# Differences of the down projection's weights, formed beside the up projection instead of beside the input projection

## The chip, the cores and the metric

The kernel runs on one core of one Trainium2 chip. A core has five engines, each with an instruction stream of its own that runs strictly in order: TensorE (PE in the profile, matrix products), VectorE (DVE), ScalarE (ACT), GpSimd (POOL) and SyncE (SP), which here issues every DMA transfer. An instruction that waits for a semaphore holds up everything behind it on its own engine. Products land in PSUM, all other tiles lie in SBUF; the large arrays lie in HBM. The metric is the device time of one execution in microseconds, as the median of several runs.

## The reference

One decoder layer over 1040 tokens of width 1024: an input projection, differential attention and an HGRN2 recurrence side by side, an output projection, and a feed-forward network with a short convolution. The last is what the change touches:

```python
def conv_ffn(a, w_up, conv_w, conv_b, w_down):
    u = a @ w_up
    C = u.shape[-1]
    u = lax.conv_general_dilated(
        u, conv_w[:, None, :].astype(u.dtype), window_strides=(1,),
        padding=[(CONV_WIDTH - 1, 0)], dimension_numbers=('NWC', 'WIO', 'NWC'),
        feature_group_count=C) + conv_b
    gate, up = jnp.split(u, 2, axis=-1)
    return (jax.nn.gelu(gate, approximate=True) * up) @ w_down
```

`w_down` has 2816 rows and 1024 columns.

## The kernel before

Every operand of a large product is split into a high part `hi` and a low remainder `lo` (`split`, lines 146 to 149: ScalarE rounds, VectorE or GpSimd subtracts), and each product is three matmuls: hi by hi, hi by lo, lo by hi.

The stages follow each other: the normalised input and first projections; then, head by head, the rest of the input projection (`dense`, line 742) interleaved with attention (`attn`) and the recurrence (`hgrn_head`); the output projection; the up projection with convolution and gate; the down projection. In the profile the input projection with its heads runs from about 52 to 500 us, the up projection from about 684 to 1150 us, the down projection to the end.

The up and the down projection each use Strassen's scheme with seven products in place of eight. It needs sums and differences of quarters of both operands. In the down projection (lines 1375 to 1548) the weights of products 5, 6, 7 and 4 are such differences. They depend on the weights alone, so they are formed ahead of time and kept in a scratch array `tsc` in HBM, from where `w_in` (line 1395) reads them. The rows of `w_down` are taken in 11 pairs of blocks of 128 rows, `k` and `k + 11`; for each `k` four tiles of 128x512 (`11`, `12`, `22`, `21`: 256 KB each) are loaded, four subtractions are made on VectorE in place, and the four results are stored. That is `down_sums` (lines 184 to 203). It is a generator: `dense` takes one step of it ahead of each group of the input projection (line 749), and the first step of a `k` loads, the next four subtract and store. Its tiles `wd` lie in the pool `wsp` with six buffers, which the output projection later uses for its weights.

The up projection runs over `ft` = 0 to 21, blocks of 128 gate columns and 128 up columns; `ft` = 0 is done without Strassen. For each other `ft` there are seven products `j` = 0 to 6, and for each of them two units `p` = 0 and 1, halves of the tokens. One unit's product is 12 matmuls. `unit` (lines 1291 to 1330) uses three PSUM banks, `pa`, `pb` and `pc`, that take several products each. Product 1 goes into `pb`, VectorE forms `u2 = pb + x1`, and product 3 adds into the same bank; then VectorE forms `u3 = pb + x1` and product 5 adds again. So product 3 waits for u2 and product 5 for u3. At the end `gated` (line 1265) runs the convolution `c` (ScalarE once, VectorE twice, for each side), the gate on ScalarE, a product on GpSimd and a store to `gsc` in HBM. `prep` (line 1078) makes the weights of the product seven places ahead: it loads four tiles `ra` for each `ft` (five buffers), forms sums `ws` on GpSimd and splits them into `uh` and `ul`, the `ul` on VectorE for `j` = 0, 1, 3, 5 and on GpSimd for `j` = 2, 4, 6.

The pool `dn` ("down", line 1360) is opened before the up projection. Its tag `gk` has four buffers of 128x512, which the down projection's `g_in` (line 1390) uses for tiles `gi` that it reads from `gsc`; the results of splitting these are `gh` and `gl`.

TensorE's order is that of the program. For the other engines and for SP's transfers a scheduler sets the order when the kernel is built: it takes the earliest instruction in program order that is ready by its own reckoning, so later work is drawn ahead where buffers are free. Through this the first four `gi` tiles of the down projection, with their `gh` and `gl`, stand in `ft` = 1 to 4 of the up projection.

## Time and profile before

| | |
|---|---|
| median of three runs | 1342.56 us (1341.45 to 1344.93) |
| the profiled execution | 1337.75 us |
| its span, first to last instruction | 1336.0 us |
| mean granted TensorE clock | 0.995 |
| TensorE busy | 1289.1 us, 96% of the span |
| VectorE busy | 909.6 us, 68% |
| ScalarE busy | 693.4 us, 52% |
| GpSimd busy | 435.4 us, 33% |
| loads of `wd`, 44 of 256 KB | issued from 52.0 to 343.8 us |
| subtractions of `wd`, 44 | from 58.1 to 352.3 us |
| stores to `tsc`, 44 of 256 KB | issued from 58.7 to 378.7 us |

Rows of the timeline give the start in us, the busy time in us, engine, line, operation, output and inputs by the program's names, their shapes and the count of instructions merged; in square brackets stands how long the engine had been idle before, and what ended that. L53 is the line of a helper that records every instruction of VectorE, ScalarE and GpSimd, so these are told apart by tiles. Rows of groups give a count, the busy time, the mean of one in ns, and the idle time ahead. Rows of waits give the total in us, the number of times and the longest. "To landing" is the time from the issue of a transfer until its semaphore shows it done. A matmul's busy time overlaps that of its neighbours.

### The profile page before, as it was taken

To read this page: it belongs to the slowest core of one execution; us is meant where nothing else is said; L and a number is where in the kernel's file an instruction comes from. 1 tells how busy PE (TensorE), PEld (TensorE's weight loads), DVE (VectorE), ACT (ScalarE), POOL (GpSimd) and SP (SyncE) were. 2 spreads that over 40 slices of the span, in tenths; PEclk is the share of its full clock that TensorE was granted. 3 is DMA by queue.
4 is the path that set the end of the run, shared out by engine and by line. 5 is a ranking of instruction groups with operands and counts; after the bars stand their busy time and mean duration, and the time that the engine had idled before them with its cause. 6 is when DMAs were issued, how large, how long until landed. Compare 5 with 4: busy or idle time off the path is not lost.

```text
span 1336.0 us, 26153 instructions
## 1 busy us (share of the span) xinstructions
PE 1289.1 (96%) x10172; PEld 1186.8 (89%) x10172; DVE 909.6 (68%) x1530; ACT 693.4 (52%) x1633; POOL 435.4 (33%) x340
## 2 busy tenths in 40 slices
PE   7999999999999998999999999999999999999997
PEld 6899999989999998677899999999999998888875
DVE  6675657574746464637798777787787776697586
ACT  7465456535654665237674454444445444454553
POOL 5211212021212110326045666656666630010121
PEclk9999999999999999999999999999999999999999
DMA  5331343144311223567512222123222225954253
GB/s 207 115 134 64 116 145 124 56 140 135 111 49 58 75 88 134 187 189 254 197 48 88 88 95 73 72 95 104 80 87 72 76 92 195 340 182 166 87 205 118
DMA packets 99425, 164.99 MB, mean 123 GB/s; under 512 B 10035, under 2 KB 34899, under 8 KB 99302
## 3 DMA queue, kind: packets, MB, share of 16 engines
q1 hardware_dynamic: 99302, 163.32, 35.9%
q8 instruction: 80, 1.31, 0.4%
q14 instruction: 43, 0.35, 0.1%
HBM read 122.65 MB, written 40.63 MB: 122 GB/s over the span
## 4 chain that ended last, share of the span: by engine, by line
PE 48%; DVE 5%; issue 3%; DMA 2%; POOL 2%; ACT 2%; SPq 0%; DVEq 0%; POOLq 0%; ACTq 0%
PE pd L1461 5%; PE pd L1462 5%; PE pd L1460 5%; PE pb L1302 4%; PE pb L1304 4%; PE pb L1303 4%; PE pc L1302 2%; PE pc L1303 2%; PE pa L1302 2%; PE pa L1304 2%; PE pc L1304 2%; PE pa L1303 2%; PE py L982 1%; PE py L978 1%; PE py L980 1%
## 5 line engine op out<-in xcount | busy, mean ns | idle before, releaser
L1302 PE MATMUL pb<-t,uh 128*128 128x258 f32 x504 | 143.0, 284 | 4.6 <-DVE u L53 4.5
L1303 PE MATMUL pb<-t,uh 128*128 128x258 f32 x504 | 141.7, 281 | 0.0
L1304 PE MATMUL pb<-t,ul 128*128 128x258 f32 x504 | 141.6, 281 | 0.0
L1461 PE MATMUL pd<-wl,gh 128*128 128x512 f32 x308 | 121.9, 396 | 0.1
L1460 PE MATMUL pd<-wh,gh 128*128 128x512 f32 x308 | 121.7, 395 | 0.0
L1462 PE MATMUL pd<-wh,gl 128*128 128x512 f32 x308 | 121.7, 395 | 0.0
L53 DVE SCALAR_TENSOR_TENSOR c<-uu,cwt,c 128x514 f32<-128x514 f32 (+1 forms) x88 | 97.0, 1102 | 20.6 <-ACT c L53 19.9
L53 POOL TENSOR_TENSOR c<-c,c 128x514 f32<-128x514 f32 (+1 forms) x44 | 63.4, 1441 | 122.7 <-ACT c L53 120.0
L1302 PEld LDWEIGHTS pb<-t,uh 128*128 128x128 f32 x504 | 95.4, 189 | 6.1 <-DVE u L53 5.8
L1303 PEld LDWEIGHTS pb<-t,uh 128*128 128x128 f32 x504 | 95.5, 189 | 0.0
L1304 PEld LDWEIGHTS pb<-t,ul 128*128 128x128 f32 x504 | 95.2, 189 | 0.0
L1302 PE MATMUL pa<-t,uh 128*128 128x258 f32 (+1 forms) x336 | 95.2, 283 | 0.0
L1304 PE MATMUL pa<-t,ul 128*128 128x258 f32 (+1 forms) x336 | 95.0, 283 | 0.0
L1303 PE MATMUL pa<-t,uh 128*128 128x258 f32 (+1 forms) x336 | 94.8, 282 | 0.0
L1302 PE MATMUL pc<-t,uh 128*128 128x258 f32 (+1 forms) x336 | 94.4, 281 | 0.0
L1303 PE MATMUL pc<-t,uh 128*128 128x258 f32 (+1 forms) x336 | 94.0, 280 | 0.0
L1304 PE MATMUL pc<-t,ul 128*128 128x258 f32 (+1 forms) x336 | 93.7, 279 | 0.0
L53 DVE SCALAR_TENSOR_TENSOR c<-ug,cwt,c 128x514 f32<-128x514 f32 (+1 forms) x88 | 86.1, 978 | 2.7 <-ACT c L53 2.0
L53 POOL TENSOR_TENSOR ul<-ws,uh 128x512 fp32r<-128x512 f32 x42 | 61.0, 1453 | 39.0 <-ACT uh L53 34.5
L1461 PEld LDWEIGHTS pd<-wl,gh 128*128 128x128 f32 x308 | 57.7, 187 | 14.9 <-DVE wl L53 1.0
L1462 PEld LDWEIGHTS pd<-wh,gl 128*128 128x128 f32 x308 | 57.7, 187 | 14.1
L1460 PEld LDWEIGHTS pd<-wh,gh 128*128 128x128 f32 x308 | 57.7, 187 | 14.0
(371 smaller groups left out, 4122.5 us busy)
## 6 DMA issues: line engine op xcount, KB each, us to landing
ra<-in_wup_dram SPq DMA_DIRECT2D x88, 256.0 KB, 2.6
mp<-msc SPq DMA_DIRECT2D x23, 512.0 KB, 5.6
wd<-in_wdown_dram SPq DMA_DIRECT2D x44, 256.0 KB, 4.3
tsc<-wd SPq DMA_DIRECT2D x44, 256.0 KB, 2.8
wi<-tsc SPq DMA_DIRECT2D x44, 256.0 KB, 2.7
gi<-gsc SPq DMA_DIRECT2D x33, 256.0 KB, 4.1
wi<-in_wdown_dram SPq DMA_DIRECT2D x33, 256.0 KB, 2.8
gsc<-c SPq DMA_DIRECT2D x22, 257.0 KB, 2.1
```

The costliest lines, as they stand in the source:

```text
L53: ins = call(*args, **kw)
L978: T.matmul(py[:r], mh, hi, start=(first and k == ks[0]), stop=False)
L980: T.matmul(py[:r], mh, lo, start=False, stop=False)
L982: T.matmul(py[:r], ml, hi, start=False, stop=(last and k == ks[-1]))
L1302: T.matmul(pt, hi[:, s], th[:, k], start=(first and k == 0), stop=False, skip_group_check=True)
L1303: T.matmul(pt, hi[:, s], tl[:, k], start=False, stop=False, skip_group_check=True)
L1304: T.matmul(pt, lo[:, s], th[:, k], start=False, stop=(k == 3), skip_group_check=True)
L1460: T.matmul(py, gh[:, s], wh, start=(k == 0 and pr not in (3, 7)), stop=False, skip_group_check=True)
L1461: T.matmul(py, gh[:, s], wl, start=False, stop=False, skip_group_check=True)
L1462: T.matmul(py, gl[:, s], wh, start=False, stop=(k == NH - 1), skip_group_check=True)
```

## The change

The differences are no longer formed beside `dense`. `down_sums` becomes a function of `k` behind the opening of the pool `dn`; its tiles come from tag `gk`, and the loop over `ft` takes three steps of it in each `ft` from 2 on, behind products 1, 3 and 5. The arithmetic, the transfers and the scratch array are the same.

```diff
-    def down_sums():
-        def load(k):
-            with tc.issue_after(last_load[-1].ins):
-                for nm, kk, half in (("11", k, 0), ("12", k, 1), ("22", k + NF // 2, 1), ("21", k + NF // 2, 0)):
-                    b[nm] = wsp.tile([P, 512], F32, tag="wd", name=f"wd{nm}_{k}")
-                    SY.dma_start(b[nm], wdown[P * kk: P * (kk + 1), 512 * half: 512 * (half + 1)])
-
-        b = {}
-        load(0)
-        yield
-        yield
-        for k in range(NF // 2):
-            for j, d, p_, q_ in ((0, "11", "12", "11"), (2, "12", "22", "12"), (1, "22", "22", "11"), (3, "21", "21", "22")):
-                V.tensor_tensor(b[d], b[p_], b[q_], op=ALU.subtract)
-                with tc.issue_after(last_load[-1].ins):
-                    SY.dma_start(tsc[j][P * k: P * (k + 1)], b[d])
-                yield
-            if k + 1 < NF // 2:
-                load(k + 1)
-                yield
-
-    wd_sums = down_sums()
...
-    def dense(tiles, preload=None, side=iter(())):
+    def dense(tiles, preload=None):
...
-                next(side, None)
...
-        interleave(dense(tiles_h, None, wd_sums), [attn(h, t_a)] + carried(), FA, 1500)
+        interleave(dense(tiles_h), [attn(h, t_a)] + carried(), FA, 1500)
...
-            interleave(dense(tiles_a, None, wd_sums), [hgrn_head(t_h)] + carried(), FH, 1500)
+            interleave(dense(tiles_a), [hgrn_head(t_h)] + carried(), FH, 1500)
...
+    def down_sums(k):
+        b = {}
+        for nm, kk, half in (("11", k, 0), ("12", k, 1), ("22", k + NF // 2, 1), ("21", k + NF // 2, 0)):
+            b[nm] = dn.tile([P, 512], F32, tag="gk", name=f"wd{nm}_{k}")
+            SY.dma_start(b[nm], wdown[P * kk: P * (kk + 1), 512 * half: 512 * (half + 1)])
+        yield
+        for j, d, p_, q_ in ((0, "11", "12", "11"), (2, "12", "22", "12"), (1, "22", "22", "11"), (3, "21", "21", "22")):
+            V.tensor_tensor(b[d], b[p_], b[q_], op=ALU.subtract)
+            SY.dma_start(tsc[j][P * k: P * (k + 1)], b[d])
+            yield
+
+    def all_sums():
+        for k in range(NF // 2):
+            yield from down_sums(k)
+
+    wd_sums = all_sums()
     for ft in range(1, NF):
         units = [unit(ft, p, ps_b) for p in range(2)]
         for j in range(7):
             prep(7 * (ft + 1) + j)
             for u in units:
                 next(u)
+            if ft > 1 and j in (1, 3, 5):
+                next(wd_sums, None)
```

## The prediction

> **What bounds the kernel now.** I read the page first, then busy time by stretches, the waits of the up projection, one period of it in order of time, and last the tiles `wd` and `tsc` that move.

> ```profile
> span 1336.0 us, 26153 instructions
> 52.00:352.00 300.00, 287.65 (x2711) 273.34 (x2711) 188.79 (x413) 162.15 (x478) 56.06 (x57) 1.00 0.37 123
> 684.00:768.00 84.00, 79.41 (x655) 78.00 (x654) 68.04 (x92) 40.85 (x74) 57.41 (x37) 1.00 0.25 89
> 768.00:900.00 132.00, 132.00 (x1113) 131.90 (x1112) 101.64 (x148) 65.22 (x115) 82.63 (x58) 1.00 0.23 83
> PE pb L1302 <- DVE u L53: 4.5, 5, 1.6
> ```

> The stretches give window, length, then busy time of PE, PEld, DVE, ACT and POOL, granted clock, DMA share, GB/s. TensorE is the bound almost everywhere: in 768 to 900, the middle of the up projection, it is busy all 132.00 us. One pass over `ft` issues 168 matmuls (14 products of 12), so it takes 168 x 132.00 / 1113 = 19.92 us. VectorE is busy 77% there, POOL 63%. In 52 to 352, where the differences are formed now, TensorE is idle 12.3 us and POOL busy only 19%. The one wait of TensorE in the whole up projection is for VectorE's `u`, 4.5 us in five pieces.

> The share of 77% looks like room. One period in order of time says how much:

> ```profile
> 898.71 0.74 DVE L53 TENSOR_TENSOR u<-pb,x 128x258 f32<-128x258 f32 x2
> 900.06 0.70 DVE L53 TENSOR_TENSOR ul<-ws,uh 128x512 fp32r<-128x512 f32 x1 [0.61 <-ACT uh L53]
> 900.92 0.43 DVE L53 TENSOR_TENSOR u<-pb,x 128x258 f32<-128x258 f32 x1 [0.16 <-PE pb L1304]
> 901.39 0.43 DVE L53 TENSOR_TENSOR uu<-pc,u 128x258 f32<-128x258 f32 x1
> 902.34 0.42 DVE L53 TENSOR_TENSOR u<-pb,x 128x256 f32<-128x256 f32 x1 [0.53 <-PE pb L1304]
> 902.80 0.42 DVE L53 TENSOR_TENSOR uu<-pc,u 128x256 f32<-128x256 f32 x1
> 905.76 0.81 DVE L53 TENSOR_TENSOR ul<-ra,uh 128x512 fp32r<-128x512 f32 x1 [2.53 <-ACT uh L53]
> 906.64 0.43 DVE L53 TENSOR_TENSOR uu<-pb,x 128x258 f32<-128x258 f32 x1
> 908.02 0.76 DVE L53 SCALAR_TENSOR_TENSOR c<-uu,cwt,c 128x514 f32<-128x514 f32 x1 [0.95 <-ACT c L53]
> ...
> 918.20 0.75 DVE L53 TENSOR_TENSOR u<-pb,x 128x258 f32<-128x258 f32 x2
> ```
> ```profile
> 899.27 0.30 PE L1302 MATMUL pb<-t,uh 128*128 128x258 f32 x1
> ```

> At 898.71 VectorE forms u2 of both units (`u<-pb,x`, two of 0.37 us); the fourth product, which adds into the same bank, starts at 899.27, just after the first is done. I call a ring the time from the end of one first u2 to the end of the next; VectorE's natural ring is 918.20 - 898.71 = 19.49 us against TensorE's 19.92: a margin of 0.4 us. The idle time in it is 0.61 + 0.16 + 0.53 + 2.53 + 0.95 = 4.78 us, all but 0.95 of it ahead of 906.64. From the `uu` at 906.64 to the end of the next first u2 (918.57) VectorE runs 11.93 us with only the 0.95 idle. So work put ahead of 906.64 has up to 3.8 us, work behind it 0.4 us.

> **The change part by part.**

> ```profile
> ra<-in_wup_dram SPq DMA_DIRECT2D x88, 256.0 KB, 2.6
> wd<-in_wdown_dram SPq DMA_DIRECT2D x44, 256.0 KB, 4.3
> tsc<-wd SPq DMA_DIRECT2D x44, 256.0 KB, 2.8
> ...
> L53 DVE TENSOR_TENSOR wd<-wd,wd x44: 671/692/1707, 58.1 to 352.3; 128x512 f32<-128x512 f32 x44
> L199 SPq DMA_DIRECT2D tsc<-wd x44: 319/404/857, 58.7 to 378.7; - x44
> DMA to landing us min/median/max: 2.0/3.6/6.0
> ...
> DMA to landing us min/median/max: 2.0/2.8/5.3
> ```
> ```profile
> L53 DVE TENSOR_TENSOR ul<-ra,uh 128x512 fp32r<-128x512 f32 x32 | 29.1, 909 | 40.5 <-ACT uh L53 40.5
> L53 DVE TENSOR_TENSOR ul<-ws,uh 128x512 fp32r<-128x512 f32 x32 | 28.3, 885 | 13.8 <-ACT uh L53 13.8
> ...
> L53 DVE TENSOR_TENSOR gl<-gi,gh 128x512 fp32r<-128x512 f32 x4 | 4.6, 1140 | 10.3 <-ACT gh L53 10.3
> ```

> What moves: 44 loads, 44 subtractions, 44 stores, eleven k of four each. The loop asks for three steps per `ft`, but the built order runs ahead: VectorE meets k = 0 in ft 1, k = 1 and 2 in ft 2, and so on to k = 9 and 10 in ft 6. TensorE's order is unchanged; POOL's and ACT's all but unchanged. In ft 2 to 6 an odd k has its first subtraction just ahead of the last convolution step before u2, the second between the two units' u2, the third and fourth behind; the even k has all four behind the second `uu<-pc,u` (902.80 in the period above). All four buffers of `gk` belong to one k, so each load of the even k waits on SP until the odd k's store from that buffer has landed.

> Prices. A subtraction: 0.69 us where it stands now; in the up projection its like (two SBUF inputs, 128x512) takes 0.885 to 0.909 with a minimum near 0.68, and `gl` 1.14. I take 0.9, bounds 0.69 and 1.14. A store's landing: 2.8, ends 2.0 and 5.3. A load's: between 2.6 (`ra`, same size, in the up projection) and 4.3 (`wd` itself, in a busier stretch), I take 3.5 as the middle; far ends 2.0 and 6.0 (these views mix tiles' loads and stores, so they are ends only). An issue on SP: 0.4.

> [...]

> One even-k ring, from the end of the first u2: second odd subtraction 0.9, u2 of the other unit 0.37, third and fourth 1.8: 3.07. Issue of the last store 0.4, its landing 2.8: 6.27. The last even load goes out then and lands 3.5 later: 9.77. The even k's last subtraction 0.9 and the queued `ul` 0.8: `uu` starts at 11.47. It started 906.64 - 899.08 = 7.56 after u2 before. Behind the subtraction, which waits on VectorE for its load, stand `ul`, `uu` and the whole convolution. Add 11.93 and the next odd k's first subtraction 0.9: 24.3 us, against 19.92. Five such rings (k = 2, 4, 6, 8, 10; in the last, `gl` takes the first subtraction's place) cost 5 x 4.38 = **+21.9**. With 0.69, 2.0 and 2.0 a ring is 20.9 (+0.9 each); with 1.14, 2.8 and 4.3 it is 26.3 (+6.4 each).

> Part of that was lost before:

> ```profile
> 700.88 0.39 PE L1302 MATMUL pb<-t,uh 128*128 128x258 f32 x1 [1.44 <-DVE u L53]
> ...
> 716.97 0.39 PE L1302 MATMUL pb<-t,uh 128*128 128x258 f32 x1 [1.58 <-DVE u L53]
> ...
> 737.78 0.39 PE L1302 MATMUL pb<-t,uh 128*128 128x258 f32 x1
> ```

> The `gl<-gi,gh` steps of the down projection, which the scheduler had drawn into ft 1 to 4, make rings of 737.78 - 716.97 = 20.81 us. The buffers they took are now taken, and they stand in ft 6 and 7: three rings give back 0.89 each, **-2.6**. At their new place three of them stand where an odd k's subtractions would with no even k behind; 4.2 us of the 5.7 that four products take: nothing.

> ```profile
> 691.28 1.25 SPq L1071 DMA_DIRECT2D ra<-in_wup_dram  x2
> ...
> 693.67 2.81 DVE L53 SCALAR_TENSOR_TENSOR c<-ug,cwt,c 128x510 f32<-128x510 f32 x2
> ...
> 700.41 0.41 DVE L53 TENSOR_TENSOR u<-pb,x 128x258 f32<-128x258 f32 x1
> ...
> 701.99 1.44 DVE L53 TENSOR_TENSOR gl<-gi,gh 128x512 fp32r<-128x512 f32 x1
> ```

> In ft 1 VectorE is without a gap up to the `u` at 700.41 that TensorE waits for. Two subtractions of k = 0 go in ahead: 1.8. The first stands at 693.67 + 1.4 = 695.1, and its second operand's load goes out behind the two `ra` loads, at 692.5, to land at 696.0: 0.9 more. Then three subtractions less one `gl` (1.44) until the wait at 716.97: 1.3. Together **+4.0** (2.0 to 6.1 at the bounds).

> Beside the input projection:

> ```profile
> 175.40 0.69 DVE L53 TENSOR_TENSOR wd<-wd,wd 128x512 f32<-128x512 f32 x1 [1.62 <-DMA wd<-in_wdown_dram]
> ...
> 177.24 0.44 PE L224 MATMUL pi_dv<-ahi,wh_dv 128*128 128x384 f32 x1 [1.74 <-ACT k L53]
> ...
> 285.89 0.69 PE L442 MATMUL pl<-hq,kr 128*32 128x16 f32 x62 [1.79 <-DVE hq L53]
> ```

> Removing 44 x 0.74 us of VectorE work returns only what TensorE waited for it. Two waits of 1.74 and 1.79 us follow a `wd` step on VectorE: **-3.5**. Bounds: 0, if something else ends the wait at the same time, and all 12.3 us of idle.

> Sum: 21.9 - 2.6 + 4.0 - 3.5 = +19.8. The profiled execution took 1337.75 us (its span is 1336.0), 4.8 below the median of the three runs, 1342.56. From its own time the sum gives 1357.6; on the median, 1362.4. I predict 1362.

> **The rivals.** *The round trip closes.* Landings near 2.0 and subtractions of 0.69: rings of 20.9, +4.6 - 2.6 + 2.0 - 3.5 = +0.5, 1343. For it: DMA share is only 0.23 to 0.25 there. [...] 10%.

> *The input projection gives back its idle time* (faster). Place: 52 to 352; price: up to 12.3 us; it decides once more than 4 us come back with the rings closed as above: 12.3 instead of 3.5 gives 1334. For it: subtractions, loads and stores all leave that stretch. Against: most of its waits end with ACT's softmax or with PSUM copies. 6%.

> *Transfers crowd.*

> ```profile
> GB/s 207 115 134 64 116 145 124 56 140 135 111 49 58 75 88 134 187 189 254 197 48 88 88 95 73 72 95 104 80 87 72 76 92 195 340 182 166 87 205 118
> ```

> A ring moves 16 transfers of 256 KB more, 172 GB/s over 24.3 us, on top of 83: some 255, where the best slice of the run reached 340. With landings of 5.3 and 6.0 a ring takes 29.3, five cost 47: 1387. 10%.

> *The clock drops.*

> ```profile
> 530.65 0.68 PE L978 MATMUL py<-woh,mp 128*128 128x512 f32 x1 [2.66 <-DVE gate L53]
> ...
> 530.00:540.00 10.00, 9.35 (x97) 7.37 (x98) 2.83 (x6) 4.22 (x8) 0.00 (x0) 0.83 0.40 144
> ```

> After a gap of 2.66 us the granted clock averaged 0.83 over 10 us: 1.7 us of work lost. Gaps of 4 us in five rings could each do that: 8.5 us, 1371. Against: the matmuls behind the gap are not what VectorE waits for next, so most of it hides. [...] 8%.

> That the change does nothing of the kind is excluded by the built order.

> **How the numbers follow.** My forecast has 66%, rings of 22 to 26.3: 1350 to 1378. The range of 1345 to 1380 takes that, the clock and half of the crowding; it leaves out most of the closed round trip (9), the faster rival (6) and the other half of crowding (5). Within 0.3% (4 us, about what a measurement can tell) lie 4 of the closed trip's 10; 2 of them are faster, with the 6 of the input projection 8; slower 88%.

> **What would show it.** Right: TensorE waits for `u` about 4 us, once in each of ft 2 to 6, and VectorE's own waits before `wd` name the DMA; 684 to 820 longer by some 23 us; 52 to 352 shorter by 3 to 4; the down projection unchanged. Wrong: waits under 1 us per ring (the landings were priced too high), waits twice as long (crowding), a clock under 1.00 in the up projection, or a gain over 6 us ahead of 400.

## The result, and the profile after

The changed kernel takes 1361.75 us (median of six runs, 1359.37 to 1364.46), the kernel before, run beside it on the same chip, 1342.30 us (six runs, 1336.17 to 1346.64). The ratio is 1.0149, with a 95% interval of 1.0126 to 1.0172: slower by 1.5%. The profiled execution took 1359.37 us, 21.6 more than that of before, and its span is 21.4 longer.

The head of the page of the kernel after, and its busy time by stretches (columns as in the prediction: window, length, busy time of PE, PEld, DVE, ACT and POOL with counts, granted clock, DMA share, GB/s):

```profile
span 1357.4 us, 26171 instructions
PE 1297.9 (96%) x10172; PEld 1196.8 (88%) x10172; DVE 923.4 (68%) x1530; ACT 693.9 (51%) x1633; POOL 439.8 (32%) x340
```
```profile
52.00:352.00 300.00, 296.12 (x2789) 283.92 (x2788) 168.98 (x386) 170.87 (x501) 56.97 (x58) 1.00 0.16 50
...
706.00:768.00 62.00, 52.38 (x403) 51.38 (x403) 56.13 (x70) 22.29 (x42) 36.21 (x23) 0.92 0.61 211
768.00:830.00 62.00, 54.47 (x430) 53.97 (x429) 53.49 (x74) 21.97 (x40) 31.70 (x22) 0.94 0.70 237
...
900.00:1150.00 250.00, 250.00 (x2032) 246.38 (x2031) 184.50 (x275) 118.62 (x209) 140.66 (x99) 1.00 0.27 94
```

Two things changed, with opposite signs. In 52 to 352 TensorE is idle 3.9 us where it was idle 12.3, and passes 2789 matmuls instead of 2711. In 706 to 830 it issues 403 and 430 matmuls per 62 us; at the 523 of the undisturbed up projection before, a fifth is missing.

TensorE's order is the same in every kernel of this study, 10172 matmuls, so the start of the n-th matmul in two traces can be compared directly. After minus before, at matmuls that stand at the given time in the trace of before:

```
at (us)             281   499   669   717   738   839   859  1099  1326
after - before     -8.5 -11.6  -9.6  -7.0  -2.2 +21.3 +21.3 +21.4 +21.4
```

The input projection gives 9.6 us up to the begin of the up projection, ft 1 takes 2.6 back, then the passes over `ft` take 28.3, and from ft 8 on nothing changes any more; the down projection is the same. The rings (from one first u2 to the next, read at the matmul that waits for it) are 25.68, 26.05, 25.74, 25.18 and 26.36 us; before, the same five took 20.81, 20.83, 20.97, 20.03 and 19.93.

The waits in the up projection after (total, times, longest), TensorE's and VectorE's:

```profile
PE pb L1279 <- DVE u L53: 25.0, 9, 4.8
```
```profile
DVE wd L53 <- DMA wd<-in_wdown_dram: 10.1, 8, 1.9
```

And one ring of the kernel after in order of time, VectorE, then GpSimd:

```profile
735.15 0.41 DVE L53 TENSOR_TENSOR u<-pb,x 128x258 f32<-128x258 f32 x1
735.49 1.70 DVE L53 TENSOR_TENSOR wd<-wd,wd 128x512 f32<-128x512 f32 x1
737.11 0.41 DVE L53 TENSOR_TENSOR u<-pb,x 128x256 f32<-128x256 f32 x1
737.44 3.11 DVE L53 TENSOR_TENSOR wd<-wd,wd 128x512 f32<-128x512 f32 x2
740.48 1.77 DVE L53 TENSOR_TENSOR ul<-ws,uh 128x512 fp32r<-128x512 f32 x1
...
745.78 2.87 DVE L53 TENSOR_TENSOR wd<-wd,wd 128x512 f32<-128x512 f32 x4 [1.94 <-DMA wd<-in_wdown_dram]
748.57 0.68 DVE L53 TENSOR_TENSOR ul<-ra,uh 128x512 fp32r<-128x512 f32 x1
749.17 0.42 DVE L53 TENSOR_TENSOR uu<-pb,x 128x258 f32<-128x258 f32 x1
...
761.21 0.41 DVE L53 TENSOR_TENSOR u<-pb,x 128x258 f32<-128x258 f32 x1
```
```profile
736.60 1.72 POOL L53 TENSOR_TENSOR ul<-ws,uh 128x512 fp32r<-128x512 f32 x1
738.40 1.61 POOL L53 TENSOR_TENSOR ws<-ra,ws 128x512 f32<-128x512 f32 x1
740.09 1.62 POOL L53 TENSOR_TENSOR ws<-ra,ra 128x512 f32<-128x512 f32 x1
```
```profile
L53 DVE TENSOR_TENSOR wd<-wd,wd x44: 677/693/1712, 686.8 to 825.4; 128x512 f32<-128x512 f32 x44
...
DMA to landing us min/median/max: 2.0/3.2/5.6
```

The four subtractions of the even k take 2.87 us, 0.7 each: GpSimd is idle beside them, from 744.9 to 751.1. The three of the odd k behind the first u2 take 1.70, 1.42 and 1.65, side by side with GpSimd's sums and splits, which take 1.6 to 1.7 as well (others of the same kinds in the up projection take 1.3). Over all 44, the 22 that overlap a GpSimd instruction by more than 0.1 us take 1.40 us on average, four of them only 0.68; the other 22 take 0.69.

The even k's subtractions waited for their loads like this (SyncE, in the same ring):

```profile
737.22 3.69 SPq L1350 DMA_DIRECT2D tsc<-wd  x3
740.99 3.29 SPq L1346 DMA_DIRECT2D wd<-in_wdown_dram  x4
```

The loads stand behind the odd k's stores in SyncE's order, and the last of these stores goes out when the last odd subtraction ends, at 740.55. VectorE waits only for the second of the four loads, 4.2 us from issue to landing.

### The profile page after: what moved, and what is told of

It is laid out like the page before. It is cut to its first block, busy times and chain, and to the rows that moved or that the text cites. A ratio compares the mean times of both kernels' runs of the same rounds, so it can differ in the third digit from the quotient of the medians.

```text
span 1357.4 us, 26171 instructions
## 1 busy us (share of the span) xinstructions
PE 1297.9 (96%) x10172; PEld 1196.8 (88%) x10172; DVE 923.4 (68%) x1530; ACT 693.9 (51%) x1633; POOL 439.8 (32%) x340
## 4 chain that ended last, share of the span: by engine, by line
PE 45%; DVE 7%; DMA 5%; ACT 3%; issue 3%; POOL 2%; SPq 1%; DVEq 0%; ACTq 0%; POOLq 0%
PE pd L1457 5%; PE pd L1458 5%; PE pd L1456 5%; PE pb L1279 3%; PE pb L1281 3%; PE pb L1280 3%; DMA wd<-in_wdown_dram 2%; PE pa L1279 2%; PE pa L1281 2%; PE pa L1280 2%; PE pc L1279 2%; PE pc L1280 2%; PE pc L1281 2%; DVE wd L53 2%; DVE c L53 1%
## 5 line engine op out<-in xcount | busy, mean ns | idle before, releaser
L1279 PE MATMUL pb<-t,uh 128*128 128x258 f32 x504 | 148.2, 294 | 25.1 <-DVE u L53 25.0
L1280 PE MATMUL pb<-t,uh 128*128 128x258 f32 x504 | 146.1, 290 | 0.0
L1281 PE MATMUL pb<-t,ul 128*128 128x258 f32 x504 | 145.7, 289 | 0.0
L1279 PEld LDWEIGHTS pb<-t,uh 128*128 128x128 f32 x504 | 100.2, 199 | 27.1 <-DVE u L53 27.1
L53 DVE SCALAR_TENSOR_TENSOR c<-uu,cwt,c 128x514 f32<-128x514 f32 (+1 forms) x88 | 94.8, 1078 | 20.5 <-ACT c L53 19.9
L53 POOL TENSOR_TENSOR c<-c,c 128x514 f32<-128x514 f32 (+1 forms) x44 | 66.9, 1522 | 124.1 <-ACT c L53 119.5
L1280 PEld LDWEIGHTS pb<-t,uh 128*128 128x128 f32 x504 | 100.3, 199 | 0.0
L1281 PEld LDWEIGHTS pb<-t,ul 128*128 128x128 f32 x504 | 99.8, 198 | 0.0
L53 DVE SCALAR_TENSOR_TENSOR c<-ug,cwt,c 128x514 f32<-128x514 f32 (+1 forms) x88 | 86.7, 985 | 2.4 <-ACT c L53 2.0
L53 POOL TENSOR_TENSOR ul<-ws,uh 128x512 fp32r<-128x512 f32 x42 | 61.5, 1465 | 59.4 <-ACT uh L53 55.2
L53 ACT CAST uh<-ra 128x512 fp32r<-128x512 f32 x67 | 41.0, 616 | 69.2 <-PE pb L1280 50.5
L53 ACT ACTIVATE c<-uu,cbt,cwt 128x514 f32<-128x514 f32 (+1 forms) x44 | 36.0, 817 | 67.8 <-DVE uu L53 67.8
## 6 DMA issues: line engine op xcount, KB each, us to landing
ra<-in_wup_dram SPq DMA_DIRECT2D x88, 256.0 KB, 2.7
wd<-in_wdown_dram SPq DMA_DIRECT2D x44, 256.0 KB, 3.5
tsc<-wd SPq DMA_DIRECT2D x44, 256.0 KB, 2.4
wi<-tsc SPq DMA_DIRECT2D x44, 256.0 KB, 2.7
gi<-gsc SPq DMA_DIRECT2D x33, 256.0 KB, 4.1
wi<-in_wdown_dram SPq DMA_DIRECT2D x33, 256.0 KB, 3.1
```

The source lines that it names most:

```text
L53: ins = call(*args, **kw)
L1279: T.matmul(pt, hi[:, s], th[:, k], start=(first and k == 0), stop=False, skip_group_check=True)
L1280: T.matmul(pt, hi[:, s], tl[:, k], start=False, stop=False, skip_group_check=True)
L1281: T.matmul(pt, lo[:, s], th[:, k], start=False, stop=(k == 3), skip_group_check=True)
```

## The experiments

The first four ask what costs the 28 us in the up projection, VectorE's stream or the 88 transfers, and where the gain beside the input projection comes from. The three that leave subtractions out were executed once each.

**No differences at all.** Products 5, 6, 7 and 4 read rows of `w_down`.

```diff
-            if ft > 1 and j in (1, 3, 5):
-                next(wd_sums, None)
...
-            SY.dma_start(t, tsc[(5, 6, 7, 4).index(pr)][P * k: P * (k + 1)])
+            kk, half = {5: (k, 0), 6: (k + NH, 1), 7: (k, 1), 4: (k + NH, 0)}[pr]
+            SY.dma_start(t, wdown[P * kk: P * (kk + 1), 512 * half: 512 * (half + 1)])
```

> The kernel after without any differences: nothing is loaded, subtracted or stored ahead, and products 5, 6, 7 and 4 read rows of w_down as they are. It gives the floor for both places. Theory A (VectorE's own stream: the subtractions stand in the way of what TensorE waits for) and theory B (the 88 transfers delay other transfers, on SP's queue or in the DMA engines) both expect some 10 us less than before by 500 us of the span, and the up projection as before, with 4 to 5 us of waits for u (the gl steps return to ft 1 to 4): a span of 1324 to 1328. If TensorE is less than 5 us ahead at 500 us, the early gain of the kernel after was chance.

Measured: 1327.81 us, span 1325.8. Against before TensorE is 9.9 us early at the start of the up projection and stays so to the end (-9.9); its waits for `u` there are those of before. So the early gain is real, and this is the floor for any version that hides the differences wholly and leaves the down projection's first `gl` in ft 1 to 4. There they make four passes longer, 23.50, 20.82, 20.82 and 20.90 us, where a pass without them takes 21.80 in ft 1 (the last experiment but one) and 19.93 elsewhere, some 4 us in sum.

**The transfers without the subtractions, beside the up projection.**

```diff
-            V.tensor_tensor(b[d], b[p_], b[q_], op=ALU.subtract)
             SY.dma_start(tsc[j][P * k: P * (k + 1)], b[d])
```

> The kernel after without the 44 subtractions; the loads and stores stay in the up projection and tsc holds the weights undiminished. Theory A expects the waits for u in the up projection to fall from 25 us to 4 or less, and a span of 1322 to 1330. Theory B expects at least half of the waits to stay, 12 us or more, and a span over 1338.

Measured: 1338.33 us, span 1336.4, between the two theories. The first three rings are 20.03, 20.06 and 21.03 us, within 0.1 us of before's or shorter, and at most 1.1 us above the undisturbed 19.93: 88 transfers alone are not what makes 25.8. Then one ring takes 29.67. In order of time, ScalarE, VectorE and SP of this kernel:

```profile
784.41 0.62 ACT L53 CAST gh<-gi 128x512 fp32r<-128x512 f32 x1 [9.42 <-DMA gi<-gsc]
```
```profile
785.06 0.69 DVE L53 TENSOR_TENSOR gl<-gi,gh 128x512 fp32r<-128x512 f32 x1 [8.59 <-ACT gh L53]
```
```profile
772.75 3.81 SPq L1346 DMA_DIRECT2D wd<-in_wdown_dram  x4
777.90 2.71 SPq L1349 DMA_DIRECT2D tsc<-wd  x4
781.69 0.32 SPq L1387 DMA_DIRECT2D gi<-gsc  x1
```

The down projection's first `gl`, which the scheduler had drawn into this pass, stands on VectorE, and its `gh` on ScalarE, ahead of a `gi` load that goes out only behind the last k's loads and stores. VectorE is idle for 8.6 us, and TensorE waits 8.6 us for the `u` behind it. Neither theory had this; it is tried by itself further down.

**The transfers without the subtractions, beside the input projection** (the kernel before without its subtractions).

> The kernel before without the 44 subtractions; loads and stores stay beside the input projection. Theory A expects TensorE to be 7 to 11 us ahead of the kernel before at 500 us, span 1325 to 1329. Theory B expects it at most 3 us ahead, span 1333 or more.

**The kernel before with the subtractions on GpSimd.**

```diff
-                V.tensor_tensor(b[d], b[p_], b[q_], op=ALU.subtract)
+                G.tensor_tensor(b[d], b[p_], b[q_], op=ALU.subtract)
```

> The kernel before with the subtractions on GpSimd, which is busy 19% of the time there, in place of VectorE; nothing left out. Theory A expects most of what x4 gains: 5 to 10 us under the kernel before, ratio 0.993 to 0.996. Theory B expects no difference beyond 0.3%. If the longer GpSimd instructions hold up the splits of the weights or block VectorE's two-input instructions, it is slower.

Measured: 1329.79 us and a span of 1328.0 without the subtractions; 1338.69 us with them on GpSimd, a ratio to before of 0.9976 (0.9954 to 0.9998), span 1335.2. The stretch 52 to 352 of the first and of the second:

```profile
52.00:352.00 300.00, 295.81 (x2784) 283.54 (x2783) 168.93 (x386) 170.45 (x498) 57.28 (x59) 1.00 0.39 126
```
```profile
52.00:352.00 300.00, 288.20 (x2711) 273.73 (x2710) 178.25 (x371) 163.05 (x480) 111.90 (x100) 1.00 0.38 122
```

The transfers cost the input projection next to nothing: with them and without subtractions TensorE is 8.8 us early at the start of the up projection. The gain is the subtractions' time on VectorE. Moved to GpSimd, which is busy 19% there, they should have given that back, and did not: fewer VectorE instructions (371 against 386) take longer (178.25 against 168.93), a mean of 480 ns instead of 438. Up to the same matmul (499 us in the trace of before), VectorE's 623 other instructions take 318.5 us in sum here and 299.7 without the subtractions: 19 of the 32.5 us that the subtractions had held VectorE come back as longer instructions. This expectation was missed, and it is the first sign that instructions are longer with GpSimd busy beside them. VectorE still had 14 us less to do than before, and TensorE was only 0.5 us early at 669 us; what took the rest is not shown.

**One k in each of ft 2 to 12, all four subtractions in VectorE's gap.** The gap is the 2.53 us ahead of 905.76 in the prediction's period, behind the second `uu<-pc,u`; `ends` is that instruction, `marks` the first u2. The loads of the next k go out behind the stores, a whole pass ahead.

```diff
-        V.tensor_tensor(uu[:, n:2 * n], pc, u3, op=ALU.add)
+        ends[ft, p] = V.tensor_tensor(uu[:, n:2 * n], pc, u3, op=ALU.add)
...
-            if ft > 1 and j in (1, 3, 5):
-                next(wd_sums, None)
+            if 2 <= ft < 2 + NF // 2 and j == 1:
+                wd = down_sums(ft - 2)
+                with tc.issue_after((marks[ft, 1] if ft == 2 else ends[ft - 1, 1]).ins):
+                    next(wd)
+            if 2 <= ft < 2 + NF // 2 and j == 3:
+                with tc.issue_after(ends[ft, 1].ins):
+                    for _ in range(4):
+                        next(wd)
```

> The changed kernel with its steps pinned: one k in each of ft 2 to 12, its four subtractions in a row on VectorE directly behind the add into uu of the second unit (where the trace of before shows VectorE idle for 2.53 us and GpSimd busy), and the loads of the next k issued behind the stores, a whole ft ahead, so that no subtraction waits for a transfer. Theory P (a subtraction beside GpSimd's two-input work takes 1.4 to 1.7 us, not 0.69): 5.6 to 6.8 us against 2.53 of idle time and 0.43 of slack, so 11 rings of 22.6 to 23.8, span 1357 to 1370. Rival W (what lengthened the rings of the changed kernel was the wait for stores and loads alone): four of 0.69 are 2.8, all within the idle time and the slack, rings of 19.9, span 1326 to 1332.

**The same with copies.** `V.tensor_copy(b[d], b[p_])` in place of the subtraction.

> The same with each subtraction replaced by a copy of its first operand (one input in SBUF, the same output tile, the same store and the same place in the queues), so the differences are left out. Theory P: the copies keep a duration of their own of at most 0.69 us beside a busy GpSimd, four fit the idle time of 2.53 us, no ring is longer than 19.9, span 1325 to 1332. Rival (what lengthens VectorE's instructions there is the transfers into and out of the same tiles, or the row of instructions as such): the copies are lengthened to 1.4 and more and the span is that of the four subtractions within 5 us.

Measured: 1353.43 us, a ratio to before of 1.0086 (1.0064 to 1.0108), span 1350.5 with subtractions; 1341.57 us, span 1340.3 with copies. The groups of the two (min/median/max in ns):

```profile
L53 DVE TENSOR_TENSOR wd<-wd,wd x44: 681/1664/1671, 707.5 to 937.2; 128x512 f32<-128x512 f32 x44
```
```profile
L53 DVE COPY wd<-wd x44: 428/1456/1519, 708.7 to 923.5; 128x512 f32<-128x512 f32 x44
```

No VectorE wait for a load is left, and the rings are still 22.2 to 22.8 us (mean of the first ten 22.40), just under what theory P asked for (its span of 1357 to 1370 was missed by 6.5 us) and far from rival W's 19.9: four subtractions of 1.3 us on average overrun the gap. The eleventh ring and the one behind it are longer for another cause, 24.39 and 21.74 with subtractions, 24.14 and 22.70 with copies: the first `gl` stands there ahead of its `gi`, as in the second experiment. With copies TensorE waits 3.94 us for the `u` behind this row:

```profile
933.33 0.69 DVE L53 TENSOR_TENSOR gl<-gi,gh 128x512 fp32r<-128x512 f32 x1 [2.37 <-ACT gh L53]
```

The two rings hold some 6 us of the copies' span that are not the copies'. The copies missed both expectations. P said that one input would keep them at 0.69 or less; 11 of the 44 take 0.43 to 0.48 us, the other 33 take 1.40 to 1.52, and the rings are 21.15 us. In one gap the four take 4.74 us from 772.15 on, while GpSimd has one instruction behind the other from 772.38 to 776.60. So it is not only instructions with two inputs that are longer beside GpSimd; a copy between SBUF tiles is longer too.

**Two subtractions per pass.** Eleven k over ft 1 to 21: two in each of ft 1 to 20, four in ft 21, same place.

```diff
-    wd_sums = all_sums()
+    wd = down_sums(0)
+    next(wd)
...
-            if ft > 1 and j in (1, 3, 5):
-                next(wd_sums, None)
+            if j == 3:
+                with tc.issue_after(ends[ft, 1].ins):
+                    for _ in range(4 if ft == NF - 1 else 2):
+                        next(wd)
+                    if ft % 2 == 0:
+                        wd = down_sums(ft // 2)
+                        next(wd)
```

> The changed kernel with its steps spread: two subtractions in each of ft 1 to 20 and four in ft 21, pinned behind the add into uu of the second unit, loads a half or whole ft ahead. Theory P: two of 1.4 are 2.8 us against 2.53 idle and 0.43 of slack, so rings stay within 0.3 us of 19.9, the input projection's 8.5 to 10 us are kept, span 1326 to 1334, and the kernel is faster than before by 0.3 to 1.0%. Rival C (any subtraction in the up projection is paid, since its VectorE ring of 19.49 has only 0.43 us to spare): 20 rings longer by 0.69 x 2 - 0.43 = 0.95, +19, span 1345 to 1350. Rival D (the collisions make GpSimd's splits late and TensorE waits for ul): waits for ul appear in most rings, span 1335 or more.

Measured: 1330.62 us, a ratio to before of 0.9918 (0.9892 to 0.9945), span 1330.2. VectorE in one gap, and the stretch from ft 12 on:

```profile
773.57 2.45 DVE L53 TENSOR_TENSOR wd<-wd,wd 128x512 f32<-128x512 f32 x2
776.18 1.54 DVE L53 TENSOR_TENSOR ul<-ra,uh 128x512 fp32r<-128x512 f32 x1 [0.16 <-ACT uh L53]
```
```profile
900.00:1062.00 162.00, 162.00 (x1368) 162.00 (x1367) 141.33 (x195) 77.67 (x139) 112.66 (x74) 1.00 0.42 136
```

The two subtractions take 2.45 us, longer than their 1.4 alone, and fill the gap; TensorE is busy all of 162.00 us while VectorE is at 87%, and every ring from ft 3 on is 19.93 to 19.97. So subtractions that meet GpSimd cost TensorE nothing in these rings: the pair shown ends at 776.02, 0.16 us before VectorE's next instruction. What is lost is at one place: TensorE runs 9.9 us ahead of before up to 1099 us and 5.5 ahead from 1146 on. The first `gl` of the down projection are late behind ft 21's four.

**The changed kernel's order, with one and with two sets of buffers.** Eleven k pinned to the places of the changed kernel's own trace; VectorE's order differs from it in ft 1 alone. The second kernel takes its tiles in turn from two tags:

```diff
-            b[nm] = dn.tile([P, 512], F32, tag="gk", name=f"wd{nm}_{k}")
+            b[nm] = dn.tile([P, 512], F32, tag=("gk", "gh")[k % 2], name=f"wd{nm}_{k}")
```

> A control for the next run: the changed kernel with its eleven k pinned to the places that they have in its own trace (k = 0 in ft 1; in each of ft 2 to 6 an odd k around the two first u2 and an even k behind the second add into uu), one set of four buffers as before, each k's loads behind the stores of the one before. All theories: the changed kernel's own time within 4 us, span 1353 to 1361, rings of 25 to 26, VectorE's waits for wd loads some 10 us.

> The same with two sets of four buffers, odd and even k in turn, each k's loads a whole k ahead, so that no subtraction waits for a store and a load; the order on VectorE is the control's. Theory P (the ring is VectorE's stream: eight subtractions, four of them beside GpSimd, and the wait for the load as one further term): the 1.9 us of waiting in each of five rings goes and nothing else, rings of some 23.9, span 9 to 10 us below the control's. Rival W (the round trip through one set of buffers is what the up projection pays for; with it gone the subtractions fit): rings of 19.9 to 21, span 25 to 32 us below the control's. Rival N (what the wait held up is late anyway): within 3 us of the control.

Measured: 1359.93 us and span 1356.5 with one set, 1355.12 us and span 1353.3 with two. VectorE's subtractions in the up projection (busy and mean; idle ahead and what ended it), one set, then two:

```profile
L53 DVE TENSOR_TENSOR wd<-wd,wd 128x512 f32<-128x512 f32 x44 | 44.7, 1016 | 10.7 <-DMA wd<-in_wdown_dram 10.1
```
```profile
L53 DVE TENSOR_TENSOR wd<-wd,wd 128x512 f32<-128x512 f32 x44 | 51.3, 1166 | 1.0 <-DMA wd<-in_wdown_dram 0.3
```

The round trip through one set of buffers was not what the rings paid for: without it they are 25.06 us on average instead of 25.78. The waits went (10.1 to 0.3 us), but the subtractions, now earlier by that much, meet GpSimd more often and take 6.6 us more. 9.8 less 6.6 is 3.2, and the five rings are 3.6 us shorter in sum. VectorE's idle time in a ring falls from 2.9 us to 1.2 while TensorE still waits for `u`: what is left is its stream of instructions. By its size that is nearest to rival N, but for a reason that none of the three had: the wait had kept the first subtraction of each even k clear of GpSimd (0.69 us; now 1.70 to 1.73).

**Ten k spread, the last one in its old place** beside the input projection, so that ft 21 has none.

> As the spread version (two subtractions in each of ft 1 to 20, behind the second add into uu), but the last k, whose four subtractions stood in ft 21 ahead of the down projection's first gl, is formed beside the input projection in its old place. Theory P: the 4.2 us that the spread version lost where the down projection begins stay away, and four subtractions beside the input projection cost a tenth of what 44 did, about 1 us: span 1325 to 1329, 2 to 4 us below the spread version. Rival: the loss at the start of the down projection comes from somewhere else (its loads), and the span is the spread version's or 1 us more.

Measured: 1333.31 us, ratio 0.9945 (0.9922 to 0.9969), span 1329.6: no better. The gain at 1099 us was already down to 6.0. ScalarE, VectorE and TensorE in ft 20, in the order of cause:

```profile
1063.31 0.62 ACT L53 CAST gh<-gi 128x512 fp32r<-128x512 f32 x1 [4.88 <-DMA gi<-gsc]
```
```profile
1063.96 0.69 DVE L53 TENSOR_TENSOR gl<-gi,gh 128x512 fp32r<-128x512 f32 x1 [3.32 <-ACT gh L53]
```
```profile
1071.02 0.39 PE L1302 MATMUL pb<-t,uh 128*128 128x258 f32 x1 [3.69 <-DVE u L53]
```

The span is the one that the rival gave, for a cause that it did not have. With buffers of `gk` free again, the scheduler drew `gh` and `gl` into ft 20, and they wait there for the load of `gi` with the convolution behind them, as in the second experiment. The cost at the start of the down projection had gone, as theory P said, and came back at another place. So the last two kernels take that one thing away, each from a kernel that had it:

```diff
-        split(gh, gl, a, V)
+        if pr == 1 and k < 4:
+            with tc.issue_after(acts[NF - 1, 1].ins):
+                A.copy(gh, a)
+            with tc.issue_after(ends[NF - 1, 1].ins):
+                V.tensor_tensor(gl, a, gh.bitcast(F32), op=ALU.subtract)
+        else:
+            split(gh, gl, a, V)
```

**Transfers without subtractions, `gl` held back** (`acts` is ScalarE's copy into `x1`).

> The changed kernel without the 44 subtractions but with their loads and stores (as in the second experiment), and the first four gh and gl of the down projection, which the scheduler had drawn forward to ft 6, held behind the work of ft 21 on ScalarE and VectorE. If the stall of 8.6 us in ft 6 came from a gl standing on VectorE ahead of its load (and gh on ScalarE), it goes: span 1325 to 1329, some 9 us below the 1336.4 of that experiment, no wait of TensorE for u longer than 1.5 us in ft 2 to 21. Rival (the transfers delay a wait that TensorE needs wherever gl stands): a stall of the same size stays, span 1333 or more.

**Ten k spread, `gl` held back.**

> As the version with ten k spread over ft 1 to 20 and the last k beside the input projection, and the first four gh and gl of the down projection held behind ft 21's work, so that none stands on VectorE ahead of its load in ft 20. Theory P: the stall of 3.7 us for u in ft 20 and the half clock behind it go, span 1324 to 1328, 2 to 5 us below that version. Rival: gl comes late for the down projection instead and TensorE waits 2 to 4 us for gl at its start, span 1328 to 1332.

Measured: 1324.89 us, span 1322.8, 13.6 below the second experiment and 2.2 below what was expected; and 1327.30 us, ratio 0.9899 (0.9876 to 0.9922), span 1324.4, 5.2 below the version with ten k. The waits of TensorE in the up projection, of the second experiment, then of the two:

```profile
PE pb L1279 <- DVE u L53: 10.9, 3, 8.6
```
```profile
PE pb L1279 <- DVE u L53: 3.7, 3, 1.4
```
```profile
PE pb L1302 <- DVE u L53: 3.8, 2, 3.3
```

The stall is gone in both. Of the transfers alone, two passes of 21.3 us remain, some 3 us in sum. The 3.3 us left in the last kernel stand in ft 1, behind the first two subtractions: VectorE has no gap there, and the pass takes 24.26 us where the version without subtractions takes 21.80. From ft 2 to ft 20 every pass takes 19.92 to 20.06. The last kernel is faster than the kernel before by 1.0% and as fast as the one that forms no differences (1327.81), which has its `gl` in ft 1 to 4, however; a kernel without differences whose `gl` are held back was not tried, and an estimate from the passes above puts it some 4 us lower.

## Why the prediction was right, and where two of its steps were not

The forecast of 1362 us and its sign held. Its sum of +19.8 stands against +21.6 of the profiled executions. Two terms were off by 6 to 7 us each, with opposite signs: that the time came within 1 us is luck, and the working is less good than the time.

- *The even-k ring, predicted 24.3, measured 25.8 on average*: five of them 7.1 us more than the sum had with `gl`'s part (+26.4 against 21.9 - 2.6). The mechanism was right in outline: odd subtractions on VectorE, loads behind them on SyncE, VectorE waiting for a load once in each ring, and `uu` with the whole convolution queued behind. In the ring shown, `uu` starts 13.6 us after the end of the first u2 (735.56 to 749.17) where the prediction had 11.47; from there to the end of the next first u2 (761.62) it is 12.45, where it had 12.83. The first mis-sized term is the subtraction at 0.9: the three odd ones with the u2 between take 4.99 us (735.56 to 740.55) instead of 3.07. The mean over all 44 is 1.04, but no subtraction of the odd k in this ring costs that: they cost 0.7 or 1.4 to 1.7, by where GpSimd stands. The prediction took its 0.9 from the means of 0.885 to 0.909 of like instructions, and those were means over other places of the ring. The second: all four even subtractions ran behind the wait, 2.87 us, where only the last was put there. The third has the other sign: the store's landing of 2.8 was not in the path. In four of the five rings the only load that VectorE waited for was the second, which went out 0.9 us after the last odd subtraction, behind a store's issue and not its landing; from the end of that subtraction to the first even one it was 5.2 us (740.55 to 745.78), where store and load together had 6.7 in the sum.
- *Input projection, predicted -3.5, measured -9.6.* The step that failed counted only two TensorE waits that directly follow a `wd` step. The runs show that most of the idle time there hung on VectorE: 8.5 of 12.3 us came back in 52 to 352, and 8.2 of them with the transfers kept and only the subtractions gone (295.81 us busy). Its own sign for being wrong, a gain over 6 us ahead of 400, was there. The faster rival's premise (idle time given back by the input projection) was right and its other half, closed rings, was not. Through which of ScalarE's and VectorE's steps 32.5 us of subtractions cost TensorE 9 to 10 was not followed further. Kernels with the same program up to there were 8.2 to 11.7 us early at 669 us, so this term is known to about 2 us.
- *ft 1, predicted +4.0, measured +2.6*: right in sign, inside its bounds of 2.0 to 6.1.
- *`gl` at its new place: nothing.* True of the changed kernel, whose `gl` stand where an odd k would with no even k behind. But the step had no price for a `gl` that waits for its `gi`, and in three experiments (the second, the copies, the ten k) TensorE waited 3.7 to 8.6 us behind just that.
- *The round trip closes.* It was judged by landings; the median landing (3.2) was near the 2.8 and 3.5 of the sum. The pinned pair shows why this rival did not come true at these places even with the waits gone: they fell from 10.1 to 0.3 us, the subtractions ran into GpSimd and rose from 44.7 to 51.3, and the rings stayed at 25.06.
- *Transfers crowd.* Not seen: landings of at most 5.6 us, and the transfers alone, with `gl` held back, leave the rings from ft 2 on at 19.9 to 21.3.
- *The clock drops.* It did, in every long wait, so a second sign for being wrong was there, a clock under 1.00 in the up projection. It cost less than the rival's 8.5 us:

```profile
735.60:739.00 3.40, 3.38 (x15) 3.38 (x16) 3.37 (x4) 0.72 (x2) 3.32 (x3) 0.50 0.63 235
...
838.80:843.00 4.20, 4.05 (x19) 4.05 (x20) 4.20 (x5) 0.85 (x2) 4.12 (x3) 0.50 0.44 142
```

These are stretches of the kernel after right behind the first of the five rings' waits (4.11 us) and the last (4.78 us); the clock granted is 0.50. In the rings the slow matmuls end before VectorE's next result does: TensorE still waits 3.3 to 4.8 us for it. Behind the last, where no such wait follows, the next ring takes 21.85 instead of 19.93: 1.9 us.

## What to carry to other kernels

An engine that is busy 77% has room only where its gaps are: find the gap in one period, measure it, and put there no more than fits at the duration that the work has beside its neighbour (here 1.40 us on average beside GpSimd), not at its duration alone (0.69). Work that is moved must also be spread; eleven groups in six periods cost 31 us, the same instructions two per period lengthened none from ft 3 to ft 20. And when a scheduler draws later work forward, look at what it draws into the buffers and idle places that a change leaves: one instruction waiting for its load at the head of an in-order queue cost up to 8.6 us.

## What was not expected of the hardware

A wait's length did not decide whether the clock fell. In the version with two subtractions per pass a wait of 2.23 us at the start of the down projection was followed by matmuls at half speed:

```profile
1106.22 0.50 PE L1460 MATMUL pd<-wh,gl 128*128 128x512 f32 x1 [2.23 <-DVE gl L53]
...
1107.84 0.63 PE L1460 MATMUL pd<-wh,gl 128*128 128x512 f32 x1
1108.27 0.63 PE L1458 MATMUL pd<-wh,gh 128*128 128x512 f32 x1
...
1111.14 0.40 PE L1459 MATMUL pd<-wl,gh 128*128 128x512 f32 x1
```

They start 0.43 us apart there, and again 0.23 to 0.24 once it is over, some 3.4 us later. In the last version a wait of 3.25 us was followed by full speed at once:

```profile
708.52 0.39 PE L1302 MATMUL pb<-t,uh 128*128 128x258 f32 x1 [3.25 <-DVE u L53]
708.75 0.28 PE L1303 MATMUL pb<-t,uh 128*128 128x258 f32 x1
```

The traces show where the two differ. In each of them the clock changes only at steps of 3.41 us from one another, the same steps from start to end; in the kernel after it falls at 733.78 and 836.18, for example, 30 steps apart. Cut at these steps, the two waits look like this, first the one of 2.23 us, then the one of 3.25 (columns as in the prediction):

```profile
1104.18:1107.59 3.41, 1.37 (x6) 1.14 (x7) 3.41 (x5) 1.71 (x4) 1.31 (x1) 1.00 0.25 90
1107.59:1111.00 3.41, 3.41 (x10) 2.64 (x9) 3.30 (x4) 1.14 (x2) 1.55 (x1) 0.50 1.01 289
```
```profile
703.37:706.78 3.41, 1.90 (x17) 1.70 (x15) 3.37 (x6) 2.11 (x4) 1.35 (x1) 1.00 0.27 82
706.78:710.19 3.41, 1.67 (x14) 1.67 (x15) 2.87 (x5) 1.66 (x3) 2.12 (x3) 1.00 0.36 131
```
